# A two-layer HGRN2 and Conformer trunk on one core: weight casts gated in the inner units of the first MLP, and TensorE in written order across the seam ahead of it

## The chip, the core and the metric

The kernel runs on one core of one Trainium2 chip. The metric is the device time in microseconds (us) of one execution; the median of several runs counts. TensorE (PE) multiplies matrices, VectorE (DVE) and ScalarE (ACT) do elementwise work, GpSimd (POOL) and SyncE (SP) mostly start transfers here. Each engine has its own queue of instructions and takes it in order; an instruction waits where data of another engine is not there yet, and whatever stands behind it in that queue waits with it.

## What is computed

All arrays are float32: 1024 tokens, model width 1024, two layers. Cut to what matters:

```python
mix = hgrn2_mixer(x, ...)                                   # layer 0; layer 1: a Conformer convolution
x = layer_norm(DEEPNORM_ALPHA * x + mix, ln_mix_g[i], ln_mix_b[i])
ff = jnp.square(jax.nn.relu(x @ ffn_w1[i])) @ ffn_w2[i]     # width 1024 -> 4096 -> 1024
x = layer_norm(DEEPNORM_ALPHA * x + ff, ln_ffn_g[i], ln_ffn_b[i])
```

The HGRN2 mixer ends with an output projection, `o @ w_out`. The change lies between that projection of layer 0 and the first matrix of its MLP (the seam), and in the rest of that first matrix.

## The kernel before

**Splitting.** A float32 matrix is split into a high part, which ScalarE casts (`nc.scalar.copy`, L72 for weights, L1045 for inputs), and a low part, which VectorE subtracts from it. A product is three matmuls for each block of 128 rows: high by high, high by low, low by high (`product`, L335). A slot of 8 KB holds both parts of a 128 x 1024 block of weights.

**Forms.** The first MLP's up-projection multiplies blocks of matrices with 7 products in place of 8. Input and weights are combined into seven forms each, numbered 1 to 7; `ORDER` is 1, 2, 6, 5, 7, 3, 4. There are eight inner units `c` of the weights; each takes its seven forms in this order (`Up.form`, L1252), and one form of one unit is 2 x 12 matmuls of 512 columns. The input forms are kept in SBUF as `xf[1]` to `xf[7]`, which the order names `x1f1` to `x1f7`. The weight forms are made by `Forms.unit` (L130) from four blocks `a0` to `a3` of a unit: form 6 is `a0 + a2 + a3`, form 5 is `a2 + a3`, form 7 is `a0 + a2`, form 3 is form 6 plus `a1`, form 4 is `a3`. The weights of forms 1 and 2 of the units 0 and 1 are brought ahead of the rest (`early`, L1141) and used before it: the program runs (unit 0, form 1), (0, 2), (1, 1), (1, 2), and then the forms 6, 5, 7, 3, 4 of unit 0 and of unit 1 (L1460 to L1474). The slot at 144 KB holds the weights of (1, 2) first, and then those of (0, 6), the first form that `fw` makes (L1454).

**The seam.** The projection is computed for two halves of 512 tokens, each with four blocks `t` of 128 tokens and two halves `n` of the columns: 24 matmuls `ps<-w,oT` for each (`t`, `n`), 384 in all. Three of them, (0, 0), (1, 0) and (2, 0) of the first half, are multiplied ahead of the rest (`early_out`, L1026). VectorE adds each to the residual `y`. When both column halves of a block are there, `x1_block` (L1194) runs its norm: two statistics, an aggregate, a power on POOL (L518), and two passes of 1024 columns on VectorE. Then TensorE transposes the block in two groups of four (`ps<-ident,y`) into the two banks of `aux`. For the first half `turn` (L1096) splits the result into `xf[1]` and `xf[2]`. For the second half `x1_first` and `x1_second` (L1173, L1180) make the forms 5, 6, 7, 3 and 4 of the block from it, eight operations of 512 columns on VectorE; forms 7, 3 and 4 are kept unsplit and are split later, in pairs of 1024 columns, by `x1_late` (L1190), behind a small copy on POOL that needs the low part of the weight form at the head of the queue.

**What sets the order.** Up to the end of the HGRN2 stage all engines keep the order in which the program is written (`manual_schedule`, L371, closed at L1038). From there a scheduler orders the instructions of each engine by its own simulated clock. In the written program the transposes are `chores`: `product` runs one chore behind itself (L335 to L343), in the order in which they were appended. The chores of the last block, `x1_first(3)` and `x1_second(3)`, are appended at L1458, behind one empty chore. The scheduler is free to move them, and to move matmuls of the projection ahead of the last steps of the recurrence.

**Casts of weights split ahead.** From unit 0 on, `spare` (L1434) uses idle engines to split 38 blocks of weights of later stages. One call casts the block that the call before loaded (ScalarE, L1443), subtracts (VectorE), stores both parts, and starts the next load into the same buffer `next`, behind a copy on POOL (L1450) that needs the low part of the weight form just made. It is called from `Forms` in the first MLP's up-projection (13 of the casts lie there) and from `Slots` in the down-projection.

Of the kernel before, what the change touches and what calls it, by code (L numbers as in the profile page):

```python
# [21 lines left out]
NTB = HT // P  # L22
# [14 lines left out]
KBYTES = 220  # L37
PAIRS = [("q", 0), ("q", 1), ("q", 2), ("q", 3), ("g", 0), ("q", 4), ("q", 5), ("q", 6), ("g", 1), ("q", 7), ("g", 2), ("g", 3)]
NPOOL = (12, 11)
SEQ = "P00 P01 P02 P03 P04 P05 P06 P07 P10 P11 P12 P13 N0 P14 F0 P15 S0 P16 P17 UA0 UA1 E2 E3 N1 E4 F1 E5 E6 S1 E7 UB0 UB1 L2 L3 L4 L5 L6 L7"  # L40


# [169 lines left out]
class Background:  # L212


    def __init__(self):
        self.jobs, self.pooled, self.chores = [], [], []
        self.pe, self.dve, self.pool, self.margin, self.hold = [0.0], [0.0], [0.0], 0.0, False

    def pump(self):
# [19 lines left out]
    def flush(self, job):  # L239
        for jobs in (self.pooled, self.jobs):  # L240
            while job in jobs:
                self.step(jobs)

    def chore(self):
        if self.chores:
# [23 lines left out]
def body(ctx, tc, d, out):  # L269
# [27 lines left out]
    def slots(kbs, name):  # L297
        return ring(kbs, (2, 1024), name, F32R)

    def raws(kbs, name="raw"):  # L300
        return ring(kbs, (1024,), name)
# [33 lines left out]
    def product(ps, parts, start=True):  # L335

        n = len(parts)
        for i, ((lh, ll), (rh, rl)) in enumerate(parts):
            tensor.matmul(ps, lh, rh, start=start and i == 0, stop=False, skip_group_check=not start)
            tensor.matmul(ps, lh, rl, start=False, stop=False, skip_group_check=not start)  # L340
            tensor.matmul(ps, ll, rh, start=False, stop=i == n - 1, skip_group_check=not start)
        bg.chore()
        bg.pump()  # L343

# [691 lines left out]
    tick(100)  # L1036
    assert not waiting and not loaded and not to_load and not gates, (waiting, gates)
    order.close()  # L1038
    oT = [o[0] for o in oT]


# [152 lines left out]
    def x1_block(half, t):  # L1194
        norm(y[half][:, t, :], g, b)
        keep(half, t, y[half][:, t, :])
        if half == 0:
            bg.chores += [lambda k=k: turn(y[0][:, t, :], xf[1 + k // 4], t, k, 4) for k in (0, 4)]
            return
        if t == 0:  # L1200
            bg.done()
            late_x.update({i: view(kb, (4, HT), F32, "xl") for i, kb in ((7, 176), (3, 184))})
        if t < NTB - 1:
            bg.chores += [lambda: x1_first(t), lambda: x1_second(t)]

    for half in range(2):
        for t, n in early_out + ((0, 1), (1, 1), (3, 0), (2, 1), (3, 1)) if half == 0 else [(t, n) for t in range(NTB) for n in range(2)]:
            ps = acc()
            if half or (t, n) not in early_out:
                product(ps, wide(oT[half], t, ws[n]))  # L1210
            yv = y[half][:, t, n * HT : (n + 1) * HT]
            vector.scalar_tensor_tensor(out=yv, in0=yv, scalar=ALPHA, in1=ps, op0=ALU.mult, op1=ALU.add)
            if n == 1:
                if half == 1 and t == 0:
                    early[0].ahead(1)
                x1_block(half, t)
                if half == 0 and t:
                    bg.chore()
    for e in early[1:]:
        e.ahead(2)  # L1220

# [209 lines left out]

    hold, staged = [], []

    def spare(after):  # L1434

        if not hold:
            return
        slot, raw = hold
        now = stat.tile([P, 2, 4], F32, tag="ss", name="ss")[:, 0, :1]
        nc.vector.tensor_copy(out=now, in_=after)  # L1440
        if staged:
            key = staged.pop()
            nc.scalar.copy(out=slot[:, 0].bitcast(F32R), in_=raw)  # L1443
            vector.tensor_tensor(out=slot[:, 1].bitcast(F32R), in0=raw, in1=slot[:, 0], op=ALU.subtract)
            ready[key] = tuple(dram.tile([P, 1024], F32, name=f"ready{len(ready)}_{i}") for i in range(2))
            for i in range(2):
                nc.sync.dma_start(out=ready[key][i], in_=slot[:, i])
        if ahead:
            name, at = ahead.pop(0)
            nc.gpsimd.tensor_copy(out=raw[:, :1], in_=now)  # L1450
            nc.sync.dma_start(out=raw, in_=d[name][at])
            staged.append((name, at))

    fw = Forms(nc, vector, slots((144, 152, 48, 112, 120), "fw"), raws(run(192, 4, 4)), raws(run(160, 2, 4), "sum"), spare, 3, range(44))  # L1454
    fw.todo = [[(blocks("w1q", 0, c), 2 if c < 2 else 0)] for c in range(NFC)]
    up = Up()

    bg.chores += [lambda: None, lambda: x1_first(NTB - 1), lambda: x1_second(NTB - 1)] + [lambda: None] * 3  # L1458
    bg.chores += [lambda i=i, k=k: x1_late(i, k) for i in (7, 3, 4) for k in (0, 2)]
    up.form(0, 1, early[0].take(1)[0])  # L1460
    up.form(0, 2, early[1].take(1)[0], late=True)
# [6 lines left out]
    for c in range(NFC):  # L1468
# [5 lines left out]
            up.form(c, i, f)  # L1474
        if c in (0, 2):
            block_sums(*to_sum.pop(0), f[:2, 1, :1].bitcast(F32))
        if c == 0:
            up.settle(1)
            hold += [view(208, (2, 1024), F32, "spare"), view(216, (1024,), F32, "next")]
# [478 lines left out]
```

## Time and profile before

| | us |
|---|---|
| runs | 2061.99, 2056.68, 2056.98 |
| median | 2056.98 |
| the profiled execution | 2059.69 |
| its span, first to last instruction | 2057.9 |
| busy in it: PE, DVE, ACT, POOL | 2026.5, 1487.4, 1092.0, 392.1 |

The seam lies at about 415 to 550 us of the span, the rest of the up-projection ends near 800. A row of a timeline gives the start in us, the duration, the engine, the line, the operation, out<-in with shapes, a count where equal rows were merged, and in brackets the idle time of the engine ahead of it with what ended it. A row of the waits gives the engine, what it waited for, the total in us, the number of times, and the longest. Nearly all matmuls carry the line of the helper that records them (L204), so they are told apart by the names of their tiles. PE's matmuls overlap their neighbours: a duration of 389 ns stands for a new one every 227 ns.

### The profile page before, as it was taken

The numbers are of one execution on the slowest core, as the hardware profiler recorded it, in microseconds if no ns is written. First come the engines' busy times: TensorE is split into PE (matmuls) and PEld (weight loads), VectorE is DVE, ScalarE is ACT, GpSimd is POOL, SyncE is SP. The second block draws the span as 40 slices with busy tenths as digits, with TensorE's granted clock in tenths as the row PEclk, the third lists the DMA queues.
The fourth block names the chain that finished last, engine by engine and source line by source line (L and its number), as shares of the span: only waits on it lengthen the run. The fifth ranks groups of instructions, "written<-read, shape, count | busy, mean of one in ns | idle before, by whom it ended". The sixth has DMA issues, their size and how long they took to land. (4 is left out here: it accounts for less than half of the span.)

```text
span 2057.9 us, 29631 instructions
## 1 busy us (share of the span) xinstructions
PE 2026.5 (98%) x11144; PEld 1670.6 (81%) x11144; DVE 1487.4 (72%) x1978; ACT 1092.0 (53%) x1725; POOL 392.1 (19%) x393
## 2 busy tenths in 40 slices
PE   8999999999999999999999999999999999999998
PEld 7888887788787888888888888888888887888886
DVE  8698887877966665666567898889589666754456
ACT  5456565631654555444443776488625555443343
POOL 0112222111100000000001699079110000100002
PEclk9999999999999999999999999999999999999999
DMA  4788989842689786999998854587759778995542
GB/s 187 221 200 228 261 240 252 268 187 82 180 295 307 243 286 224 372 338 325 338 336 301 308 185 184 194 330 272 255 215 343 241 231 297 392 294 197 194 154 102
DMA packets 183944, 517.55 MB, mean 251 GB/s; under 512 B 17912, under 2 KB 49784, under 8 KB 182776
## 3 DMA queue, kind: packets, MB, share of 16 engines
q1 hardware_dynamic: 168312, 456.93, 61.8%
q0 software_dynamic: 15488, 58.72, 12.3%
q8 instruction: 87, 1.43, 0.3%
q14 instruction: 57, 0.47, 0.1%
HBM read 380.85 MB, written 201.85 MB: 283 GB/s over the span
## 5 line engine op out<-in xcount | busy, mean ns | idle before, releaser
L204 PE MATMUL ps<-dw,dh 128*128 128x512 f32 x2688 | 611.1, 389 | 0.0
L204 PEld LDWEIGHTS ps<-dw,dh 128*128 128x128 f32 x2688 | 504.2, 188 | 104.6 <-DVE dh L204 0.2
L204 PE MATMUL ps<-x1f,fw 128*128 128x512 f32 x1344 | 309.7, 392 | 4.6 <-ACT c L1266 2.5
L204 PEld LDWEIGHTS ps<-x1f,fw 128*128 128x128 f32 x1344 | 252.5, 189 | 60.3 <-ACT c L1266 3.6
L204 PE MATMUL ps<-xf,fs 128*128 128x512 f32 x1008 | 250.0, 399 | 3.7 <-issue 2.0
L204 POOL TENSOR_TENSOR cb<-cb,prod 128x512 f32<-128x512 f32 x168 | 223.1, 1337 | 12.5 <-ACT prod L1589 2.0
L204 DVE TENSOR_TENSOR dh<-dh 128x1024 fp32r<-128x1024 f32 x112 | 136.5, 1222 | 116.1 <-ACT dh L72 112.7
L204 PEld LDWEIGHTS ps<-xf,fs 128*128 128x128 f32 x1008 | 185.1, 189 | 43.3 <-issue 2.2
L204 DVE SCALAR_TENSOR_TENSOR ps<-u,par,ps 128x512 f32<-128x512 f32 x296 | 206.1, 749 | 11.0 <-ACT ps L1601 9.5
L204 PE MATMUL ps<-xa,wa 128*128 128x512 f32 x864 | 203.0, 392 | 0.1
L72 ACT CAST dh<-dh 128x1024 fp32r<-128x1024 f32 x112 | 117.4, 1051 | 156.0 <-DMA dh<-hf 148.9
L204 PEld LDWEIGHTS ps<-xa,wa 128*128 128x128 f32 x864 | 160.3, 188 | 33.2 <-ACT ha L1331 0.3
L72 ACT CAST dw<-dr 128x1024 fp32r<-128x1024 f32 x112 | 117.3, 1052 | 131.0 <-PE ps L204 115.3
L204 DVE TENSOR_TENSOR dw<-dr,dw 128x1024 fp32r<-128x1024 f32 x112 | 136.3, 1222 | 69.5 <-ACT dw L72 68.4
L1589 ACT ACTIVATE prod<-u,par 128x512 f32<-128x512 f32 x168 | 119.8, 726 | 37.1 <-POOL cb L204 36.7
L518 POOL TENSOR_TENSOR mv<-mv,nhalf 128x1 f32<-128x1 f32 x32 | 42.2, 1321 | 404.8 <-DVE mv L204 394.5
L1450 POOL COPY next<-ss 128x1 f32<-128x1 f32 x38 | 18.9, 497 | 414.5 <-DVE spare L204 255.1
L204 PE MATMUL ps<-w,oT 128*128 128x512 f32 x384 | 89.9, 392 | 1.3 <-ACT oT L932 0.8
L204 PE MATMUL ps<-xb,wa 128*128 128x512 f32 x384 | 91.1, 393 | 0.0
L204 DVE TENSOR_TENSOR spare<-next,spare 128x1024 fp32r<-128x1024 f32 x38 | 46.5, 1224 | 60.4 <-ACT spare L1443 60.3
L204 PE MATMUL ps<-vw,xf 128*128 128x512 f32 x336 | 79.9, 400 | 5.9 <-ACT vw L435 5.3
L204 PEld LDWEIGHTS ps<-w,oT 128*128 128x128 f32 x384 | 71.4, 188 | 16.6 <-ACT oT L932 1.2
(249 smaller groups left out, 2955.9 us busy)
## 6 DMA issues: line engine op xcount, KB each, us to landing
wa<-ready SPq DMA_DIRECT2D x140, 512.0 KB, 4.6
dh<-hf SPq DMA_DIRECT2D x112, 512.0 KB, 5.0
sum_w<-in_w_dram POOLq DMA_DIRECT2D x40, 1024.0 KB, 10.6
ready<-spare SPq DMA_DIRECT2D x76, 512.0 KB, 5.3
raw<-in_w1q_dram SPq DMA_DIRECT2D x66, 512.0 KB, 4.4
dr<-sum_w SPq DMA_DIRECT2D x64, 512.0 KB, 5.7
hf<-ht SPq DMA_DIRECT2D x112, 256.0 KB, 5.1
dr<-in_w_dram SPq DMA_DIRECT2D x48, 512.0 KB, 4.6
```

What stands on the lines that cost most here:

```text
L72: self.nc.scalar.copy(out=slot[:, 0, c], in_=raw[:, c])
L204: return op(*args, **kw)
L518: nc.gpsimd.tensor_tensor(out=dst, in0=src, in1=nhalf[:, :n], op=ALU.pow)
L1450: nc.gpsimd.tensor_copy(out=raw[:, :1], in_=now)
L1589: nc.scalar.activation(tp, u[:, k : k + HT], AF.Copy, scale=tap(j, k))
```

## The change

TensorE alone is put back under the written order right behind L1038, and stays there until unit 1 of the up-projection is done. So that the written order has the transposes at a useful place, they are no longer chores: `bg.soon` notes them with a due time 8.0 us later on a clock that counts TensorE's matmuls (35 matmuls), and `product` looks for due ones after every three matmuls. Each block's two groups now come together. The last block is treated as the others. In `spare`, called from the up-projection's `Forms`, a copy of one column on POOL into the slot of the high part now stands ahead of the cast, and needs the low part of the weight form just made; the down-projection's calls stay as they were.

```diff
+LAG_NORM = 8.0
...
+    def soon(self, us, *jobs):
+        self.due.append((self.pe[0] + us, jobs))
+
+    def dues(self):
+        while self.due and self.due[0][0] <= self.pe[0]:
+            for job in self.due.pop(0)[1]:
+                job()
...
             tensor.matmul(ps, ll, rh, start=False, stop=i == n - 1, skip_group_check=not start)
+            bg.dues()
...
     order.close()
+    order.enter_context(tc.manual_schedule(engines={mybir.EngineType.PE}))
...
         if half == 0:
-            bg.chores += [lambda k=k: turn(y[0][:, t, :], xf[1 + k // 4], t, k, 4) for k in (0, 4)]
+            bg.soon(LAG_NORM, lambda: turn(y[0][:, t, :], xf[1], t, 0, 4), lambda: turn(y[0][:, t, :], xf[2], t, 4, 4))
             return
         if t == 0:
-            bg.done()
+            assert not bg.due
...
-        if t < NTB - 1:
-            bg.chores += [lambda: x1_first(t), lambda: x1_second(t)]
+        bg.soon(LAG_NORM, lambda: x1_first(t), lambda: x1_second(t))
...
-                if half == 0 and t:
-                    bg.chore()
...
-    def spare(after):
+    def spare(after, late_cast=False):
...
         if staged:
             key = staged.pop()
+            if late_cast:
+                nc.gpsimd.tensor_copy(out=slot[:, 0, :1], in_=now)
             nc.scalar.copy(out=slot[:, 0].bitcast(F32R), in_=raw)
...
-    fw = Forms(nc, vector, ..., spare, 3, range(44))
+    fw = Forms(nc, vector, ..., lambda after: spare(after, True), 3, range(44))
...
-    bg.chores += [lambda: None, lambda: x1_first(NTB - 1), lambda: x1_second(NTB - 1)] + [lambda: None] * 3
+    bg.chores += [lambda: None] * 6
...
+        if c == 1:
+            order.close()
```

How the instructions move. First TensorE at the end of the recurrence, before; `ident,o` are the transposes of the last head's two halves, `xf_505` and `xf_432` are products of the last pair, `w,oT` is the projection.

```order
L204 MATMUL ps<-xf_505,fs 128x512 x6
L204 MATMUL ps<-w,oT 128x512 x6
L204 MATMUL ps<-ident,o 128x128 x4
L204 MATMUL ps<-xf_432,fs 128x512 x6
L204 MATMUL ps<-w,oT 128x512 x6
L204 MATMUL ps<-ident,o 128x128 x4
L204 MATMUL ps<-xf_432,fs 128x512 x6
L204 MATMUL ps<-w,oT 128x512 x145
L204 MATMUL ps<-ident,y 128x128 x8
```

The same place now.

```order
L205 MATMUL ps<-xf_505,fs 128x512 x6
L205 MATMUL ps<-ident,o 128x128 x4
L205 MATMUL ps<-xf_432,fs 128x512 x6
L205 MATMUL ps<-ident,o 128x128 x4
L205 MATMUL ps<-xf_432,fs 128x512 x6
L205 MATMUL ps<-w,oT 128x512 x132
L205 MATMUL ps<-ident,y 128x128 x8
```

The twelve projection matmuls that the scheduler had put between the transposes of `o` stand behind them again; the first transposes of `y` stand 36 matmuls behind the product that their norm needs (96 of the 132).

Second, TensorE where the up-projection goes from form 2 of unit 1 to the forms that `fw` makes, before; `fw_4501` holds the weights of (1, 2), `fw_5044` and `fw_5043` those of the forms 5 and 6 of unit 0.

```order
L204 MATMUL ps_70<-x1f2_4509,fw_4501 128x512 x24
L204 MATMUL ps_70<-x1f5_4505,fw_5044 128x512 x2
L204 MATMUL ps_70<-x1f6_4504,fw_5043 128x512 x4
L204 MATMUL ps_70<-x1f5_4505,fw_5044 128x512 x22
L204 MATMUL ps_70<-x1f6_4504,fw_5043 128x512 x20
```

Now, where the names have moved by one or two: `fw_4503` is (1, 2), `fw_5045` and `fw_5046` are the forms 6 and 5 of unit 0.

```order
L205 MATMUL ps_70<-x1f2_4511,fw_4503 128x512 x24
L205 MATMUL ps_70<-x1f6_4506,fw_5045 128x512 x24
L205 MATMUL ps_70<-x1f5_4507,fw_5046 128x512 x24
L205 MATMUL ps_70<-x1f7_4512,fw_5049 128x512 x24
L205 MATMUL ps_70<-x1f3_4508,fw_5051 128x512 x24
```

Form 6 now follows (1, 2) with nothing between.

Third, VectorE at the same place, before, from the first sum of unit 0's blocks on; `c1` are the evacuations of (1, 2), `x1f` the late input forms, `fw` the low parts of weight forms.

```order
L204 TENSOR_TENSOR sum_5058<-raw_5054,raw_5055 128x1024
L204 TENSOR_TENSOR fw_5050<-raw_5055,fw_5050 128x1024
L204 TENSOR_TENSOR c1_5145<-c1_5145,ps_70 128x512
L204 TENSOR_TENSOR sum_5059<-sum_5058,raw_5052 128x1024
L204 TENSOR_TENSOR raw_5054<-raw_5052,raw_5054 128x1024
L204 TENSOR_TENSOR c1_5146<-c1_5146,ps_70 128x512
L204 TENSOR_TENSOR fw_5044<-sum_5058,fw_5044 128x1024
L204 TENSOR_TENSOR fw_5043<-sum_5059,fw_5043 128x1024
```

Now, from the same sum on; the second `sum_5060` is the first sum of unit 1.

```order
L205 TENSOR_TENSOR sum_5060<-raw_5056,raw_5057 128x1024
L205 TENSOR_TENSOR sum_5061<-sum_5060,raw_5054 128x1024
L205 TENSOR_TENSOR raw_5056<-raw_5054,raw_5056 128x1024
L205 TENSOR_TENSOR fw_5046<-sum_5060,fw_5046 128x1024
L205 TENSOR_TENSOR fw_5052<-raw_5057,fw_5052 128x1024
L205 TENSOR_TENSOR fw_5049<-raw_5056,fw_5049 128x1024
L205 TENSOR_TENSOR c1_5147<-c1_5147,ps_70 128x512
L205 TENSOR_TENSOR x1f3_4508<-xl_4796,x1f3_4508 128x1024 x2
L205 TENSOR_TENSOR c1_5148<-c1_5148,ps_70 128x512
L205 TENSOR_TENSOR x1f4_4514<-x4_4490,x1f4_4514 128x1024 x2
L205 TENSOR_TENSOR sum_5060<-raw_5056,raw_5057 128x1024
L205 TENSOR_TENSOR fw_5045<-sum_5061,fw_5045 128x1024
```

The low part of form 6 (`fw_5043`, now `fw_5045`) stood second behind the last `c1`; now the two late pairs `x1f3` and `x1f4`, the low parts of the forms 4 and 7 and unit 1's sum stand ahead of it.

More of the change, by code (lines that the diff above doesn't have):

```diff
@@ L215, in __init__ @@
     def __init__(self):
-        self.jobs, self.pooled, self.chores = [], [], []
+        self.jobs, self.pooled, self.chores, self.due = [], [], [], []
         self.pe, self.dve, self.pool, self.margin, self.hold = [0.0], [0.0], [0.0], 0.0, False
@@ L1452, in spare @@
             staged.append((name, at))
-    fw = Forms(nc, vector, slots((144, 152, 48, 112, 120), "fw"), raws(run(192, 4, 4)), raws(run(160, 2, 4), "sum"), spare, 3, range(44))
+    fw = Forms(nc, vector, slots((144, 152, 48, 112, 120), "fw"), raws(run(192, 4, 4)), raws(run(160, 2, 4), "sum"), lambda after: spare(after, True), 3, range(44))
     fw.todo = [[(blocks("w1q", 0, c), 2 if c < 2 else 0)] for c in range(NFC)]
     up = Up()
-    bg.chores += [lambda: None, lambda: x1_first(NTB - 1), lambda: x1_second(NTB - 1)] + [lambda: None] * 3
+    bg.chores += [lambda: None] * 6
     bg.chores += [lambda i=i, k=k: x1_late(i, k) for i in (7, 3, 4) for k in (0, 2)]
```

## The prediction

> **What bounds the kernel now.** I read the page's busy shares first, then TensorE's waits by stretch, then the timeline of the stretches that the edit touches.
>
> ```profile
> PE 2026.5 (98%) x11144; PEld 1670.6 (81%) x11144; DVE 1487.4 (72%) x1978; ACT 1092.0 (53%) x1725; POOL 392.1 (19%) x393
> ```
>
> TensorE is busy 2026.5 of 2057.9 us, so the whole kernel has 31 us of idle TensorE, and an edit that only reorders can win a part of these or add to them. TensorE's waits in three stretches (seam, then the inner units of the first MLP):
>
> ```profile
> PE ps L204 <- ACT fw L72: 1.5, 1, 1.5
> PE ps L204 <- DVE c L204: 0.3, 1, 0.3
> ...
> PE ps L204 <- ACT c L1266: 1.8, 2, 1.3
> ...
> PE ps L204 <- ACT c L1266: 0.5, 1, 0.5
> PE ps L204 <- DVE c L204: 0.2, 1, 0.2
> ```
>
> The first two lie at 420 to 545 us (the seam), the third at 620 to 700, the last two at 700 to 800. So the seam wait is 1.8 us and the inner units lose 2.5 us. That is all that these two edits can remove directly.
>
> The idle costs more than its length. Windows (start:end, length, PE busy, count, granted clock, DMA share, GB/s) and two rows of the PE timeline:
>
> ```profile
> 347.45 1.08 PE L204 MATMUL ps<-xf,fs 128*128 128x512 f32 x4 [2.02 <-issue]
> ...
> 350.00:352.00 2.00, 2.00 (x6) 0.50 1.06 248
> ...
> 536.86 0.70 PE L204 MATMUL ps<-x1f,fw 128*128 128x512 f32 x2 [0.28 <-DVE c L204]
> 539.04 11.19 PE L204 MATMUL ps<-x1f,fw 128*128 128x512 f32 x41 [1.48 <-ACT fw L72]
> ...
> 540.00:542.00 2.00, 2.00 (x6) 0.50 0.46 135
> 542.00:544.00 2.00, 2.00 (x8) 0.66 1.04 383
> ```
>
> After 2.02 us of idle, and after 0.28 + 1.48 = 1.76 us, the granted clock stood at 0.50 for about 3.4 us (540 to 542 wholly, 542 to 544 at 0.66, which is 1.36 us at half), so each lost 1.7 us more. After 1.25 us (659 us, below) it did not.
>
> **Part 1, TensorE in written order at the end of the recurrence.** In the trace:
>
> ```profile
> 413.28 1.62 PE L204 MATMUL ps<-xf,fs 128*128 128x512 f32 x6
> 415.70 0.73 PE L204 MATMUL ps<-w,oT 128*128 128x512 f32 x2 [0.80 <-ACT oT L932]
> 416.96 1.20 PE L204 MATMUL ps<-w,oT 128*128 128x512 f32 x4 [0.52 <-DVE oT L204]
> 417.99 0.60 PE L204 MATMUL ps<-ident,o 128*128 128x128 f32 x4
> ...
> 421.54 1.64 PE L204 MATMUL ps<-xf,fs 128*128 128x512 f32 x6
> 423.01 33.06 PE L204 MATMUL ps<-w,oT 128*128 128x512 f32 x145
> 455.91 1.03 PE L204 MATMUL ps<-ident,y 128*128 128x128 f32 x8
> 456.70 6.39 PE L204 MATMUL ps<-w,oT 128*128 128x512 f32 x27
> ```
>
> The unit costs: (455.91 - 423.01) / 145 = 0.227 us for a matmul, 456.70 - 455.91 = 0.79 us for eight transposes. Now the order puts the four transposes of `o` directly behind the six matmuls that start at 413.28, whose slots end at 414.65. What they wait for:
>
> ```profile
> 416.05 1.16 ACT L741 ACTIVATE o<-ps,ss 128x128 f32<-128x128 f32 x4
> ...
> 418.52 1.20 ACT L741 ACTIVATE o<-ps,ss 128x128 f32<-128x128 f32 x4
> ...
> 423.90 0.69 DVE L204 SCALAR_TENSOR_TENSOR t<-ps,sq 128x512 f32<-128x512 f32 x1 [0.90 <-ACT sq L854]
> ```
>
> These ScalarE rows stand in the same order in both programs and wait for nothing that TensorE does after 414.65. So the transposes start at 417.3 instead of a filler at 415.70: 2.65 us of idle. Four transposes (0.36) and six matmuls (1.37) bring 419.0; the next `o` is there at 419.75, 0.75 idle; then six matmuls end at 421.5. Six `w,oT` matmuls later one waits for the evacuation of the last pair's bank: 424.59 (the VectorE row's end) - 422.90 (421.54 + 6 x 0.227) = 1.7 us behind the pair's last matmul, 1.4 of them filled, 0.35 idle. So the stretch stands as if it had begun at 421.9 with nothing done. Before, it began at 423.0 with 12 matmuls done, which is as if at 420.3. Loss: 1.6 us.
>
> Idle of 2.65 us in one piece is more than the 2.02 that halved the clock, so I take a half clock at about 417 to 420.5. It overlaps the 0.75 and part of the 0.35 above and adds only 0.7: the stretch begins as if at 422.6.
> [...]
>
> **Part 2, the transposes 35 matmuls behind their norm.** Number the matmuls from there, so that 384 end the output projection. For the first half nothing waits: from its add of 478.95 (rows below) to the end of its last step a norm takes 482.42 + 1.28 - 478.95 = 4.75 us, and 35 matmuls take 8. In the second half VectorE also does the eight form steps for each token block. Its order up to the first matmul with a low part of form 6 (after matmul 482) decides. From the add of block 3, columns 0, which needs matmul 360, VectorE's new order holds 18 operations of 1024 columns, 24 of 512 or of that cost, and two tiny ones. Rows for the prices (VectorE timeline):
>
> ```profile
> 478.95 0.68 DVE L204 SCALAR_TENSOR_TENSOR y<-y,ps 128x512 f32<-128x512 f32 x1
> ...
> 482.42 1.28 DVE L204 SCALAR_TENSOR_TENSOR y<-y,mv,ln_mix_b 128x1024 f32<-128x1024 f32 x1 [0.44 <-POOL mv L518]
> ...
> 529.37 0.69 DVE L204 TENSOR_TENSOR y<-y,x1f 128x512 f32<-128x512 f32 x1
> 530.10 0.69 DVE L204 SCALAR_TENSOR_TENSOR y<-y,ps 128x512 f32<-128x512 f32 x1
> 530.75 0.69 DVE L204 TENSOR_TENSOR x1f<-y,x1f 128x512 fp32r<-128x512 f32 x1
> 531.36 0.68 DVE L204 SCALAR_TENSOR_TENSOR x<-y,x1f 128x512 f32<-128x512 f32 x1
> ...
> 545.29 4.63 DVE L204 TENSOR_TENSOR x1f<-xl,x1f 128x1024 fp32r<-128x1024 f32 x4 [1.16 <-ACT x1f L1045]
> ```
>
> 4.63 / 4 = 1.16 us each for 1024 columns; starts 0.73 apart where one needs the one before and 0.61 where not, I take 0.63 for 512. So 18 x 1.16 + 24 x 0.63 = 36.0, plus 0.35 for the two tiny ones, 0.45 for the POOL power in the last norm and 0.2 for the last transposes: 37.0 us in which VectorE has no gap to give. TensorE reaches matmul 360 at 422.6 + 360 x 0.227 + 6 x 0.79 = 509.1, VectorE starts 0.2 later, and the low part is there at 546.3; TensorE takes it at 546.4. TensorE alone would be at matmul 480 at 422.6 + 109.0 + 8 x 0.79 = 537.9. On the way the last group of transposes waits for its norm, by the same count some 1.4 us; this wait lies inside the 37.0.
>
> The cause at the end is one queue. Form 6's weights go into the slot that form 2 of unit 1 still reads; before, TensorE spent two matmuls of form 5 there and waited 1.48 us. Now ScalarE's cast of form 6 stands behind four casts of late input forms, and VectorE's low part stands behind `c1`, the `x1f4` pair and the next unit's sum. `c1` itself waits for matmul 480. So even a VectorE that is on time needs 0.6 + 2 x 1.16 + 1.14 + 1.22 + 0.3 = 5.6 us behind matmul 480, and TensorE has two matmuls (0.45) to put there: at least 5.1 us idle, against 1.76 before.
>
> In the trace two matmuls of the new form were done at 539.04. So this place is reached 546.4 - 539.04 = 7.4 us later, part 1 included. The half clock behind it was there before (1.7 us) and I take the same. Behind it, forms 5, 7, 3, 4 have 24 matmuls (5.5 us) each, and VectorE catches up.
>
> **Part 3, the gated casts.** Rows at the longest wait, ScalarE and TensorE, then a VectorE row, then ScalarE's waits at 560 to 780:
>
> ```profile
> 656.68 1.05 ACT L1443 CAST spare<-next 128x1024 fp32r<-128x1024 f32 x1 [4.28 <-DMA next<-in_wpw_dram]
> ...
> 659.21 3.06 PE L204 MATMUL ps<-x1f,fw 128*128 128x512 f32 x12 [1.25 <-ACT c L1266]
> ...
> 708.09 1.23 DVE L204 TENSOR_TENSOR spare<-next,spare 128x1024 fp32r<-128x1024 f32 x1 [5.06 <-ACT spare L1443]
> ...
> ACT spare L1443 <- DMA next<-in_wpw_dram: 29.3, 10, 4.3
> ```
>
> ScalarE takes its queue in order: it held the copy of `c`, and so TensorE, behind a cast whose weights had not landed. The gate puts the cast behind a POOL copy that needs the low part of the current form; by then the load of one `spare` call earlier is long in. ScalarE then waits for VectorE's copy and POOL's, about 1 us, and a copy of `c` has a whole form (5.5 us) of cover. The added POOL copies cost POOL little (19% busy). Queued behind the cast are VectorE's `spare` subtract, which now stands one or two rows behind its gate and idles VectorE some 1.6 us each time, and the stores on SP; before, VectorE waited up to 5.06 us for the same cast. I take the full 2.5 us gain; bounds 0 and 2.5.
>
> **The sum.** +7.4 - 2.5 = +4.9 us. The profiled execution took 2059.69 (span 2057.9), 2.7 above the median of the runs, 2056.98; nothing in the sum scales with that, so a profiled execution would take 2064.6 and the median 2062. A measurement of this kernel tells about 0.3% (6.2 us) from no change: below 2050.8 or above 2063.2.
>
> **The rivals.**
> - *The clock stays full at 417*: a gap of 2.65 us does not halve it, part 1 costs 1.6 instead of 2.3, and the time is 2061.3. For it: the 0.80 + 0.52 us of idle at 415.70 did not. Against: 2.02 did. Chance 0.12. [...]
> - *VectorE is on time at the seam*, since single operations overlap better than my 0.63 and 1.16. Then only the floor holds: part 1 with 2.3, the seam 5.1 - 1.76 = 3.3, the casts -2.5: +3.1, and 0.7 less if the clock stays full; 2059.8. Against it: VectorE's starts in the quoted rows are as tight as its durations. Chance 0.18.
> - *A load is late, the slower side.* The next unit's sum, which now stands ahead of form 6's low part, needs two blocks whose buffers come free only with the low parts of forms 4 and 7, at about 538. Until 544, when VectorE reaches the sum, is 6 us. From a landing of over 6 us every microsecond goes straight to TensorE. DMA issues, KB each and median us to landing:
>
> ```profile
> sum_w<-in_w_dram POOLq DMA_DIRECT2D x40, 1024.0 KB, 10.6
> ...
> raw<-in_w1q_dram SPq DMA_DIRECT2D x66, 512.0 KB, 4.4
> ```
>
>   The loads in question are the second row; the first, of 1 MB, goes out next to them and is the upper end. So up to +4.6, taken as +3, 2065. Chance 0.20.
> - *The gate wins nothing*: ScalarE waits for POOL as long as it did for the load. Then 2064.5. Against it: POOL is idle there. Chance 0.10.
> - Both edits help and the seam wait vanishes (1.76 + 1.7 + 2.5 = 6.0 us, 2051): the order of VectorE excludes it, 0.02.
>
> **The numbers.** The forecast has 0.38 (2060 to 2063.5; 0.06 of it above the bound). Slower by over 0.3%: 0.06 + 0.20 + 0.10 = 0.36. Faster: 0.02. The rest, 0.62, is within 0.3%. Range: the forecast, the clock's rival and the gate's (0.60), most of the on-time case and half of the late load (0.23): 2057.5 to 2066.5.
>
> **What would show it.** TensorE's timeline after: transposes of `o` with some 2.6 us of idle on ScalarE ahead of them; a granted clock of 0.5 behind them; one wait of 1 to 2 us at the last group of `ident,y` on VectorE; at the first matmuls of form 6 two waits, on ScalarE's cast and on VectorE's low part, together 5 to 7.5 us; no wait for `c` over 0.5 us after 620. The forecast is wrong if the seam's two waits are under 4 us together, or if ScalarE's waits at the gated cast bring TensorE's `c` waits back.

## The result and the profile after

| | before | after |
|---|---|---|
| median of the runs, us | 2058.55 (22 runs, 2054.10 to 2065.14) | 2063.74 (22 runs, 2059.63 to 2071.63) |
| profiled execution, us (span) | 2059.69 (2057.9) | 2063.70 (2061.9) |

The ratio of after to before is 1.0023 (95% interval 1.0015 to 1.0032): 4.7 us slower, inside the 0.3% that one measurement can hardly tell. The forecast was +4.9 us and 2062.0, range 2057.5 to 2066.5. The median of before is 1.6 us above that of the three runs shown first, so it is the difference that compares.

TensorE's timeline of after (start, length, operation, and in brackets the idle time ahead of it and what ended it):

```profile
416.11 0.66 PE L205 MATMUL ps<-ident,o 128*128 128x128 f32 x4 [2.36 <-ACT o L751]
...
421.42 30.49 PE L205 MATMUL ps<-w,oT 128*128 128x512 f32 x132
...
525.13 1.09 PE L205 MATMUL ps<-ident,y 128*128 128x128 f32 x8 [1.59 <-DVE y L205]
525.98 13.87 PE L205 MATMUL ps<-x1f,fw 128*128 128x512 f32 x60
542.60 0.73 PE L205 MATMUL ps<-x1f,fw 128*128 128x512 f32 x2 [2.75 <-ACT fw L73]
546.64 13.74 PE L205 MATMUL ps<-x1f,fw 128*128 128x512 f32 x52 [3.31 <-DVE fw L205]
```

The four foretold waits are there: 2.36 us for the last head's output (2.65 in the forecast, which counted from the end of a matmul's slot and not from the end of its row), 1.59 at the last transposes, 2.75 + 3.31 at form 6. Windows of after (start:end, length, busy TensorE, count, granted clock, DMA share, GB/s) show a half clock behind the first, and another that began at about 543.4 us, inside the last two waits (542 to 544 us has 0.85), and went on behind them:

```profile
416.00:418.00 2.00, 1.89 (x9) 0.78 1.00 389
418.00:420.00 2.00, 2.00 (x8) 0.50 1.03 422
...
546.00:548.00 2.00, 1.36 (x3) 0.50 0.86 240
548.00:550.00 2.00, 2.00 (x6) 0.50 1.04 307
```

VectorE's timeline of after, the two ends of the chain that was counted at 37.0 us: from the add of block 3 at 509.00 to the end of form 6's low part at 546.59 it is 37.6.

```profile
509.00 0.69 DVE L205 SCALAR_TENSOR_TENSOR y<-y,ps 128x512 f32<-128x512 f32 x1 [0.57 <-PE ps L205]
...
541.96 2.35 DVE L205 TENSOR_TENSOR x1f<-x,x1f 128x1024 fp32r<-128x1024 f32 x2
...
545.37 1.22 DVE L205 TENSOR_TENSOR fw<-sum,fw 128x1024 fp32r<-128x1024 f32 x1
```

In the inner units, 560 to 840 us, TensorE's waits came down to one row; ScalarE's at the casts (in total, times, longest) moved from the load to GpSimd. The forecast had about 1 us for each; they took 24.2 / 7 = 3.5 us on average:

```profile
PE ps L205 <- DVE c L205: 0.2, 1, 0.2
```

```profile
ACT spare L1453 <- POOL spare L1452: 24.2, 7, 6.8
...
ACT spare L1453 <- DMA next<-in_wpw_dram: 8.1, 3, 4.6
```

**How single profiles are compared here.** The part ahead of 412 us is the same in all these kernels, yet from one execution to the next it ends up to 9 us apart. So I use two distances that don't hang on it. A goes from the moment when the last head's scaled output is ready (where TensorE starts its transposes; in the scheduler's order 0.06 us behind the end of ScalarE's row) to the third matmul of form 6 in unit 0. B goes from there to the first matmul of the down-projection (`dw,dh`). Where form 6 starts without a wait, its third matmul is worked out: 62 matmuls of 0.227 us (13.87 us less the 0.48 that one takes to drain, over 59) behind the start of the row that follows the last transposes, or 53 with the longer lag.

| kernel | A | B | A+B against before | timed ratio, 95% interval |
|---|---|---|---|---|
| before | 121.8 | 288.8 | | |
| after | 130.5 | 284.7 | +4.6 | 1.0023 (1.0015 to 1.0032) |
| casts only | 121.8 | 286.7 | -2.2 | 0.9990 (0.9978 to 1.0002) |
| written order only | 130.6 | 284.1 | +4.1 | 1.0019 (1.0007 to 1.0031) |
| after, later `o` | 129.7 | 284.9 | +3.9 | 1.0013 (1.0001 to 1.0024) |
| after, slots exchanged | 123.5 | 289.6 | +2.5 | 1.0000 (0.9989 to 1.0012) |
| after, 44 matmuls | 125.5 | 287.0 | +1.9 | 1.0002 (0.9991 to 1.0012) |
| both repairs (slots, later `o`) | 123.0 | 285.1 | -2.5 | 0.9983 (0.9971 to 0.9995) |
| slots exchanged, no gate | 123.6 | 291.2 | +4.1 | 1.0014 (1.0002 to 1.0026) |
| both repairs, sums later | 123.0 | 283.4 | -4.3 | 0.9975 (0.9963 to 0.9987) |
| before, gate, sums later | 121.8 | 286.6 | -2.3 | 1.0008 (0.9995 to 1.0020) |
| both repairs, sums later, 44 | 121.5 | 284.2 | -4.9 | 0.9977 (0.9966 to 0.9987) |
| both repairs, sums later, no gate | 123.1 | 290.4 | +2.9 | 1.0019 (1.0008 to 1.0031) |
| the same, load's copy on VectorE | 123.0 | 283.7 | -4.0 | 0.9986 (0.9975 to 0.9998) |

A+B, from one profile each, follows the timed ratio (0.001 is 2.1 us) within about 2.5 us in all rows but one, taken up below. So after's 4.7 us are A + 8.8 and B - 4.1. A half clock of 3.41 us in one of these distances makes it 1.7 us longer: before and after both have one behind the start of form 6, in B; casts only (granted clock 1.00 from 536 to 552 us), both repairs, both repairs with the sums later (with 35 and with 44 matmuls) and the last row (in these four a matmul every 0.227 us from the last transposes on) have none.

### The profile page after: what moved, and what is told of

Its sections match the earlier page's. It is cut to its first block, busy times and chain, and to the rows that moved or that the text cites. A ratio compares the mean times of both kernels' runs of the same rounds, so it can differ in the third digit from the quotient of the medians.

```text
span 2061.9 us, 29644 instructions
## 1 busy us (share of the span) xinstructions
PE 2026.0 (98%) x11144; PEld 1672.5 (81%) x11144; DVE 1489.5 (72%) x1978; ACT 1096.1 (53%) x1725; POOL 395.7 (19%) x405
## 5 line engine op out<-in xcount | busy, mean ns | idle before, releaser
L205 PEld LDWEIGHTS ps<-xb,wa 128*128 128x128 f32 x384 | 71.1, 188 | 14.3
L205 PEld LDWEIGHTS ps<-vw,xf 128*128 128x128 f32 x336 | 64.6, 193 | 20.4 <-ACT vw L445 5.3
```

The source lines that it names most:

```text
L205: return op(*args, **kw)
```

## The experiments

**Each half alone.** Casts only is the kernel before with this edit alone; written order only is after without it:

```diff
+            if late_cast:
+                nc.gpsimd.tensor_copy(out=slot[:, 0, :1], in_=now)
             nc.scalar.copy(out=slot[:, 0].bitcast(F32R), in_=raw)
```

> The kernel before with the gate on the casts and nothing else. In the trace of after, the stretch from the third matmul of form 6 in unit 0 to the first matmul of the down-projection took 831.3 - 546.6 = 284.7 us, against 827.9 - 539.0 = 288.9 before: 4.2 us less, where the forecast had 2.5. Theory A, the gate alone does this: the stretch takes 284.7, no wait for c over 0.3 us after 620 us, and the time is 4.2 us (0.2%) below before, a ratio of 0.998. Theory B, the gate is worth the 2.5 us of listed waits and the other 1.7 us came with TensorE's written order: the stretch takes 286.4, ratio 0.9988. Rival C, the gate wins nothing since ScalarE waits for GpSimd instead: the stretch takes 288.9, ratio 1.000.

> The changed kernel without the gate on the casts: only TensorE's written order and the later transposes. Theory A: form 6's third matmul in unit 0 at 546.6 as in after, 7.6 us later than before; the waits for c come back (2.8 us listed) and the stretch to the down-projection takes 288.9, so the time is 7.6 us above before, ratio 1.0037. Theory B: the stretch takes 287.2, plus 5.9 us, ratio 1.0029. Rival: with TensorE in written order the units no longer wait for c at all, the stretch takes 284.7 and the time is that of after, plus 3.4 us.

TensorE's timeline of written order only, from 540 to 840 us:

```profile
543.93 1.04 PE L205 MATMUL ps<-x1f,fw 128*128 128x512 f32 x2 [2.74 <-ACT fw L73]
547.97 284.23 PE L205 MATMUL ps<-x1f,fw 128*128 128x512 f32 x1246 [3.01 <-DVE fw L205]
832.04 8.32 PE L205 MATMUL ps<-dw,dh 128*128 128x512 f32 x36
```

Without any gate 1246 matmuls ran with no listed wait. On the written order the gate wins nothing: B is 284.1 without it, 284.7 with it, and timed 1.0019 against 1.0023, inside each other's intervals. So the 4.1 us of after's B are not the gate's; the rival named for the second run holds for B.

On the kernel before, the gate alone made B 286.7, the size of theory B. But TensorE's timeline of casts only still has the waits:

```profile
538.07 11.58 PE L204 MATMUL ps<-x1f,fw 128*128 128x512 f32 x48 [1.47 <-ACT fw L72]
551.08 108.61 PE L204 MATMUL ps<-x1f,fw 128*128 128x512 f32 x478 [1.44 <-ACT c L1266]
660.00 5.74 PE L204 MATMUL ps<-x1f,fw 128*128 128x512 f32 x24 [0.31 <-ACT c L1266]
666.83 158.06 PE L204 MATMUL ps<-x1f,fw 128*128 128x512 f32 x696 [1.09 <-DVE c L204]
```

The waits for `c` are 2.8 us here, against 2.5 listed before. Of the 2 us by which B is shorter, 1.7 are the half clock that before had behind the start of form 6 (0.50 from 540 to 542 us) and this execution did not have (1.00 there). The timed ratio, 0.9990 (0.9978 to 1.0002), can't be told from 1 either. So no run shows that the gate wins anything on the kernel before.

**Is it the place of the transposes of `o`?** They stand six matmuls later:

```diff
-            for c in range(half * NTB, half * NTB + NTB):
-                tensor.transpose(out_ps[:, c, :], o[:, c], ident)
+            def turn_out():
+                for c in range(half * NTB, half * NTB + NTB):
+                    tensor.transpose(out_ps[:, c, :], o[:, c], ident)
+                later(1, end)
...
-            later(1, end)
+            later(2 if h == H - 1 else 0, turn_out)
```

> The changed kernel with the two groups of transposes of the last head's output each put six matmuls later in TensorE's order. The forecast's part 1: what the written order costs there is the place of the transposes. Then TensorE waits 1.3 us (12 matmuls end at 416.0, the output is scaled at 417.3) and 0.75 us, the clock stays full since no gap is over 1.6 us, and the matmuls of the output projection begin at 420.1 on the scale of before instead of 421.4 in after; since VectorE's chain at the seam starts from a matmul of this projection, all of it comes 1.3 us earlier: 1.3 us below after, ratio to after 0.9994. Rival 1: the two gaps together still halve the clock: 0.6 us below after. Rival 2: something other than TensorE sets the seam's end: form 6 at the same 546.6 as in after.

TensorE's timeline of it:

```profile
414.68 0.66 PE L205 MATMUL ps<-ident,o 128*128 128x128 f32 x4 [0.98 <-ACT o L751]
...
417.18 0.66 PE L205 MATMUL ps<-ident,o 128*128 128x128 f32 x4 [0.45 <-ACT o L751]
417.60 1.62 PE L205 MATMUL ps<-w,oT 128*128 128x512 f32 x6
420.50 3.74 PE L205 MATMUL ps<-w,oT 128*128 128x512 f32 x15 [1.28 <-DVE t L205]
```

The clock stayed full there: the six matmuls behind the first wait took 1.64 us (415.09), against 2.40 in after (416.52). The stretch of the projection began 2.4 us earlier behind the output (417.60 - 414.68 = 2.9 us, against 421.42 - 416.11 = 5.3 in after); the expected 1.3 set a time of after beside one of before, whose output is ready 1.2 us later. The wait for the last pair's bank, which grew to 1.28 us, took more than half of the 2.4 back, and A fell by 0.9. So what TensorE saves at 417 does reach the end of the seam, through VectorE's start. The timed ratios, 1.0013 and 1.0023, don't settle it: their intervals overlap.

**Is it the slot, or VectorE's chain?**

```diff
-slots((144, 152, 48, 112, 120), "fw")
+slots((152, 144, 48, 112, 120), "fw")
```

> The changed kernel with the first two of the five weight slots exchanged, so that form 6 of unit 0 goes into the slot whose raw weights were cast long before, and form 5 into the one that form 2 of unit 1 reads until matmul 480. Theory: the seam's two waits (2.75 and 3.3 us) come from this slot and from what VectorE and ScalarE have queued ahead of form 6; now its low part stands ahead of both copies of c1 and is ready at about 537.5, so form 6 starts without a wait, its third matmul at about 540.2 instead of 546.6, and the half clock behind is gone: 6.4 + 1.7 = 8 us below after, ratio to before 0.9977. Form 5's low part is there at about 544.6, needed at 545. Rival 1, VectorE's chain of 37 us is the bound whatever the slots: the wait moves to form 5 or form 3, and the time is at most 3 us below after. Rival 2, the loads behind the slots come late: same, with waits on DMA in VectorE's rows.

VectorE's timeline of it, then TensorE's:

```profile
535.91 1.22 DVE L205 TENSOR_TENSOR fw<-sum,fw 128x1024 fp32r<-128x1024 f32 x1
...
542.78 1.22 DVE L205 TENSOR_TENSOR fw<-sum,fw 128x1024 fp32r<-128x1024 f32 x1
```

```profile
524.73 54.68 PE L205 MATMUL ps<-x1f,fw 128*128 128x512 f32 x240
579.84 8.47 PE L205 MATMUL ps<-x1f,fw 128*128 128x512 f32 x36 [0.44 <-ACT c L1274]
588.59 65.60 PE L205 MATMUL ps<-x1f,fw 128*128 128x512 f32 x288 [0.28 <-DVE c L205]
656.63 12.81 PE L205 MATMUL ps<-x1f,fw 128*128 128x512 f32 x48 [2.45 <-ACT c L1274]
670.51 158.05 PE L205 MATMUL ps<-x1f,fw 128*128 128x512 f32 x696 [1.07 <-DVE c L205]
```

The low part of form 6 was done at 537.1 and form 5's at 544.0, and TensorE ran on without a wait: A fell by 7.0 us, 0.5 of it because the clock also stayed full at 417 (1.00 in all windows of 2 us from 412 to 424 us). So the seam's wait came from the slot that form 2 of unit 1 still read, with what stood ahead of form 6 on ScalarE and VectorE because of it. But B rose by 4.9 us: waits for `c` of 4.2 us came back, with the gate in place. The longest, 2.45 us, stands behind VectorE: it had waited 4.87 and 2.30 us, up to 645.49 and 650.75, for stores of `ht` (`hf<-ht`), and its adds to `c`, which ScalarE needs, came late. The time fell by 0.23% where 0.46% was expected.

**Is the distance of 35 matmuls too short?**

```diff
-LAG_NORM = 8.0
+LAG_NORM = 10.0
```

> The changed kernel with the transposes 44 matmuls behind their norm instead of 35. In after, TensorE waits 1.59 us at the last group, and form 6's low part comes 37.6 us behind the add at matmul 360 with no gap on VectorE. Theory, VectorE's chain sets the seam's end: the same operations stand behind the add at matmul 360, but those that read block 2's transposes now wait for TensorE (the transposes come 9 matmuls, 2.1 us, later, at about 513.6 to 514.7 on the scale of after, where VectorE is at 512.5), so the last norm and form 6's low part come about 2 us later: the wait at the last group stays at 1.6 us, form 6's third matmul is at about 548.7 instead of 546.6, and the time is 2 us above after, ratio to before about 1.003. Rival, the distance is too short: the wait at the last group vanishes and form 6 starts 1.6 us earlier, ratio about 1.0015.

VectorE's timeline of it, then TensorE's:

```profile
513.71 0.68 DVE L205 SCALAR_TENSOR_TENSOR y<-y,ps 128x512 f32<-128x512 f32 x1
...
544.36 1.22 DVE L205 TENSOR_TENSOR fw<-sum,fw 128x1024 fp32r<-128x1024 f32 x1
545.50 2.35 DVE L205 TENSOR_TENSOR x1f<-xl,x1f 128x1024 fp32r<-128x1024 f32 x2
```

```profile
530.01 1.09 PE L205 MATMUL ps<-ident,y 128*128 128x128 f32 x8 [0.68 <-DVE y L205]
...
543.83 0.73 PE L205 MATMUL ps<-x1f,fw 128*128 128x512 f32 x2 [1.14 <-ACT fw L73]
545.63 4.60 PE L205 MATMUL ps<-x1f,fw 128*128 128x512 f32 x12 [1.07 <-DVE fw L205]
```

Both my expectation (A + 2) and its rival (A - 1.6) failed: A fell by 5.0 us. I had taken it that the same operations stand ahead of form 6's low part. They don't: with the other lag the scheduler put the pairs of late input forms (2.35 us each, the last row above) behind it, and the chain from the add of block 3 is 31.9 us (545.58 - 513.71) instead of 37.6. That VectorE's queue sets form 6's start holds; its length is a matter of order.

**Is the gain paid back in the inner units, and by whom?** Three kernels: both repairs together; the exchanged slots without the gate; and both repairs with the block sums moved:

```diff
-        if c in (0, 2):
+        if c in (4, 6):
             block_sums(*to_sum.pop(0), f[:2, 1, :1].bitcast(F32))
```

> The changed kernel with both repairs, the exchanged weight slots and the later transposes of the last head's output; the gate stays. At the seam: from the first of the six matmuls that open the end of the recurrence to the third matmul of form 6 some 126.7 us, against 134.5 in after, 127.6 with the slots alone and 125.8 before. Theory A, what the seam saves is paid back in the inner units, whose copies of c then wait for a crowded DMA: waits for c of 3 to 5 us between 560 and 690, the stretch from form 6's third matmul to the down-projection near 289, ratio to before 1.000 as with the slots alone. Theory B, the waits for c in that run were chance: the stretch is 285, ratio 0.998.

> The exchanged weight slots without the gate on the casts: neither the seam's wait nor the gate. It fills the fourth place beside after (wait and gate, waits for c 0.2 us), the written order alone (wait, no gate, 0.0 us) and the exchanged slots (gate, no wait, 4.3 us). Theory A, the units' waits for c are set by the lead that the seam's wait gives the other engines and the DMA, and the gate is worth about 2 us where there is no lead: waits for c of 5 to 7 us, the stretch from form 6's third matmul to the down-projection at 291, ratio to before 1.001. Rival, the gate itself is what holds ScalarE in the run with the exchanged slots: waits for c under 1 us, stretch 285, ratio 0.998.

> The kernel with both repairs and the gate, and the two block sums of units 0 and 2 (1 MB copies and accumulating transfers on GpSimd's and SyncE's queues) put to units 4 and 6 instead. In the run with the exchanged slots the DMA engines were at a share of 1.0 from 630 to 660 us, ahead of the wait of 2.45 us for c. Theory, the crowd of transfers is what makes the inner units wait when TensorE comes early: with these transfers gone from 560 to 680 the waits for c there fall below 1 us, the stretch from form 6's third matmul to the down-projection takes 285 or less, and the time is 4 to 5 us below the kernel with both repairs, ratio to before 0.997 to 0.998. Rival 1: the waits move to units 4 to 6 with the transfers, and the time is the same as with both repairs. Rival 2: the stores of the down-projected halves and the casts alone fill the queues: waits for c in 560 to 680 as without this edit.

Both repairs: A 123.0, waits for `c` of only 1.6 us in all, ratio 0.9983, the first version that beats the kernel before. The 4.2 us of waits with the exchanged slots alone seem to be in part the chance of that execution. Without the gate it was as theory A had it: B 291.2 and one wait of 5.65 us for `c`. VectorE's and ScalarE's timelines ahead of that wait, then ScalarE's of written order only:

```profile
653.18 0.69 DVE L205 SCALAR_TENSOR_TENSOR ht<-ht,hr 128x512 f32<-128x512 f32 x1 [5.79 <-DMA hf<-ht]
```

```profile
661.69 1.04 ACT L1453 CAST spare<-next 128x1024 fp32r<-128x1024 f32 x1 [2.77 <-DMA next<-in_wpw_dram]
```

```profile
662.40 1.05 ACT L1453 CAST spare<-next 128x1024 fp32r<-128x1024 f32 x1 [3.99 <-DMA next<-in_wpw_dram]
```

Two delays add up to the 5.65 us: VectorE's wait for a store, which held up the copies of `c`, and a late load at ScalarE's cast. Written order only has the same late cast, 0.7 us later, and TensorE did not wait, since it had come to the third matmul of form 6 5.2 us later (547.97 against 542.75). So the seam's wait is a lead that hides these delays. Beside written order only, which has no gate either, the exchanged slots took 7.0 us from A and added 7.1 to B: all of it was paid back, and the timed ratios, 1.0014 and 1.0019, don't differ. With the sums later the last waits in 560 to 690 went, B is 283.4 and the ratio 0.9975. Its interval overlaps that of both repairs, so this last step is likely, not shown.

**Three ways to the same units.** The kernel before with the gate and the sums later; the best one with the lag of 44 matmuls; and the best one without the gate.

> The kernel before, with TensorE in the scheduler's order, with the gate on the casts and the two block sums put from units 0 and 2 to units 4 and 6. Distances that don't hang on when the program's first part ends: from the last head's scaled output to the third matmul of form 6, 121.7 us in before and in casts only, 130.5 in after, 123.1 with both repairs; from there to the down-projection 288.9 in before, 286.7 in casts only, 283.3 with both repairs and the sums later. Theory, the crowd of transfers in units 0 and 2 is what makes the units wait, whatever TensorE's order: the second distance falls to 283.5 and the sum of both to 405.3, 5.3 us under before, ratio 0.9974; so the old order at the seam with these two edits is as fast as the best so far. Rival, the units are quick only in the written order: the second distance stays at 286.7, ratio 0.999.

> The kernel with both repairs, the gate and the sums later, with the transposes 44 matmuls behind their norm instead of 35. With 35 TensorE waited 1.61 us at the last group; with 44 matmuls and the old slots it waited 0.68. Theory: form 6 no longer waits in either, so this time the 0.95 us at the last group reach the seam's end: from the last head's scaled output to form 6's third matmul 122.1 us instead of 123.05, the rest as with 35, ratio to before 0.997. Rival: the later transposes push VectorE's late steps so far that form 6 or form 5 waits again: 123 us or more, ratio 0.9975 or above.

> The kernel with both repairs and the sums later, without the gate on the casts. With the sums in units 0 and 2 the gate was worth 291.1 - 289.5 = 1.6 us of the stretch from form 6's third matmul to the down-projection (exchanged slots, without and with gate). Theory A, the gate only mends what the crowd of transfers brings about, since without it the loads land before their casts are reached: the stretch is 283 to 284 as with the gate, waits for c under 0.6 us, ratio to before 0.9975. Theory B, ScalarE still stands behind a cast whose load is late once in a while: waits for c of 1.5 to 3 us, stretch 285 to 286.5, ratio 0.9985 to 0.999.

On the kernel before the later sums won no time. Its waits for `c` are 1.59 us (at 732.7, where the sums now run) instead of the 2.8 of casts only, but B is 286.6, since this execution had the half clock behind the start of form 6 (0.50 from 540 to 542 us), 1.7 us. Its timed ratio, 1.0008, is 4 us above what A+B says; that one stays open. With 44 matmuls A came down by 1.5 us, where 0.95 was foretold (121.5; the wait at the last transposes 0.36 us), but B rose by 0.9 and the time is the same. Without the gate neither theory's size held: 5.67 us of wait for `c`. The rows ahead of it show its cause. ScalarE's, GpSimd's, SyncE's and TensorE's timelines:

```profile
726.60 1.04 ACT L1455 CAST spare<-next 128x1024 fp32r<-128x1024 f32 x1 [10.67 <-DMA next<-in_wpw_dram]
```

```profile
710.24 0.86 POOL L433 DMA_DIRECT2D sum_w<-sum_w  x1 [11.74 <-DMA sum_w<-in_w_dram]
718.83 0.81 POOL L433 DMA_DIRECT2D sum_w<-sum_w  x1 [7.73 <-DMA sum_w<-sum_w]
719.37 0.46 POOL L1462 COPY next<-ss 128x1 f32<-128x1 f32 x1
```

```profile
719.86 0.34 SPq L1463 DMA_DIRECT2D next<-in_wpw_dram  x1
```

```profile
729.12 102.81 PE L205 MATMUL ps<-x1f,fw 128*128 128x512 f32 x444 [5.67 <-ACT c L1276]
```

The load `next` goes out only when GpSimd has made a copy of one column, and that copy stood in GpSimd's queue behind an accumulating transfer that waited 7.73 us for the transfer before it. The load is late, ScalarE stands at its cast, and `c` behind it. GpSimd's timeline of the kernel before has the same rows ahead of TensorE's longest wait for `c`:

```profile
644.94 0.83 POOL L423 DMA_DIRECT2D sum_w<-sum_w  x1 [7.78 <-DMA sum_w<-sum_w]
645.48 0.48 POOL L1450 COPY next<-ss 128x1 f32<-128x1 f32 x1
```

**The test of that cause.** No gate, and that copy on VectorE in the first MLP's units:

```diff
-            nc.gpsimd.tensor_copy(out=raw[:, :1], in_=now)
+            (nc.vector if late_cast else nc.gpsimd).tensor_copy(out=raw[:, :1], in_=now)
             nc.sync.dma_start(out=raw, in_=d[name][at])
```

> The kernel with both repairs and the sums later and no gate on the casts, with one more edit: the small copy ahead of each load of the next spare weights, which holds that load back, runs on VectorE instead of GpSimd, in the first MLP's units. In the run without this edit TensorE waited 5.67 us for c at 729 us: ScalarE's cast waited 10.67 us for the load, which went out at 719.9, since GpSimd's copy stood from about 710 to 719.4 behind a sum's accumulating transfer that waited 7.73 us for the transfer before it. The same row stands before the waits of 5.65 us (exchanged slots without gate) and of 1.25 us (the kernel before, GpSimd's copy at 645.5 behind a wait of 7.78). Theory, the late load comes from GpSimd's queue and not from a slow transfer: without that queue the wait at 729 goes below 1 us, the stretch from form 6's third matmul to the down-projection takes 283 to 284.5 us instead of 290.3, and the ratio to before is 0.997 to 0.998 instead of 1.0019, without a gate. Rival, the transfers themselves are slow beside the sums: the wait stays at 3 us or more, ratio 1.000 to 1.002. Rival 2: the copy on VectorE waits for ScalarE's cast of the same buffer and delays VectorE: waits for c on VectorE of over 1 us.

SyncE's, GpSimd's and TensorE's timelines of it:

```profile
707.85 0.77 SPq L1461 DMA_DIRECT2D next<-in_wpw_dram  x1
```

```profile
715.24 0.81 POOL L433 DMA_DIRECT2D sum_w<-sum_w  x1 [8.97 <-DMA sum_w<-sum_w]
```

```profile
811.44 11.17 PE L205 MATMUL ps<-x1f,fw 128*128 128x512 f32 x48 [0.83 <-ACT c L1276]
```

GpSimd's second transfer still waits 8.97 us, but the load goes out at 707.85, ahead of it. The 5.67 us are gone, B is 283.7 as with the gate, and the time went from 1.0019 to 0.9986, where 0.997 to 0.998 was expected. What is left are the 0.83 us and, outside of B, 0.76 us at the start of the down-projection. Some of the scheduler's order on VectorE changed with the edit. So this wait of 5.67 us comes from GpSimd's queue, and with the copy off that queue the kernel without a gate is as fast as the one with it, inside the intervals (0.9986 and 0.9975). Not every wait for `c` comes from there: those of 2.45 and 5.65 us with the exchanged slots stand behind VectorE's waits for stores, the second only in part. That the gate works by keeping ScalarE from standing at the late load is argued here, not shown.

## Why the prediction was right, point by point

The number was right (+4.9 against +4.7), in part by luck: the seam cost 8.8 us instead of 7.4, and the inner units gave back 4.1 instead of 2.5, two misses that cancel. The first two parts were right in mechanism, and the third was right in sign for another reason than the one given.

- *Part 1, 2.3 us.* The stretch of the output projection began 5.3 us behind the output's readiness (421.42 - 416.11). The forecast had 5.3 with the wait for the last pair's bank counted in; this wait lies inside the row of 132 matmuls, which is 30.49 us long where 131 x 0.227 + 0.48 make 30.2, so 0.3 us. The half clock cost 0.5 of the 0.7 counted: from the output to the first transposes of `y` it is 451.75 - 416.11 = 35.6 us, and 450.43 - 415.33 = 35.1 with the exchanged slots, where the clock stayed full. That it came at all was chance, as the windows below show: of the five kernels with this order at 417, all with a gap of 2.34 to 2.36 us, three had it (after, written order only, 44 matmuls: the six matmuls behind it took 2.40 to 2.81 us) and the two with the exchanged slots had not (1.64 us).
- *Part 2, the seam.* Forecast: A = 546.4 - 417.3 = 129.1; measured 130.5. From the stretch's start to VectorE's add it took 87.6 us instead of 86.7. Of this 0.3 is the bank's wait, and 0.5 are the six groups of transposes, which take 0.88 us each and not the 0.79 counted: a row of 48 matmuls has its transposes 499.76 - 488.77 = 10.99 us behind its start, 0.09 more than 48 x 0.227. The chain took 37.6 instead of 37.0. That the wait at the last transposes lies inside the chain was right as a count, but the claim that VectorE's order fixes the seam's end was too strong: with other slots, or another lag, the same work stands in another order, and 5 to 7 us go.
- *Part 3, the gated casts.* This step failed: "the full 2.5 us gain" for the gate. B fell by 4.1, and by 4.8 with no gate at all. Nor did ScalarE's waits at the casts shrink to about 1 us each: those listed above are 24.2 + 8.1 = 32.3 us, against the 29.3 for the load before. Where TensorE comes about 9 us late to form 6, loads, casts and GpSimd are that much ahead, and the waits for `c` don't arise; where it comes early they return, 0.5 to 4.2 us with the gate and 2.5 to 5.9 without. So about half of the seam's 8.8 us comes back by itself, and the two terms of my sum are not independent. The argument that GpSimd is little used (19% busy) failed too: it stood for 7 to 12 us at a time in front of a transfer, which no busy share shows.
- *The rivals.* The late load at the seam did not happen: no wait on a DMA stands in VectorE's rows there. The gate that wins nothing (0.10) came true in this kernel, with its reason: ScalarE waited as long as before. TensorE did not, because of the lead. The clock that stays full at 417 came true in other executions.

The half clock is less regular than the prediction had it. TensorE's timeline of the exchanged slots:

```profile
415.33 0.66 PE L205 MATMUL ps<-ident,o 128*128 128x128 f32 x4 [2.36 <-ACT o L751]
```

The same 2.36 us that halved the clock in after did not here (1.00 from 412 to 424 us), and the 0.28 + 1.48 us that halved it in before did not in casts only (0.28 + 1.47, and 1.00 from 536 to 552 us).

Four traces show where half clocks begin. In each, those that can be placed begin whole multiples of 3.413 us apart: at 348.79 and 539.93 us in before (56 of them), at 348.85, 417.12 and 543.41 in after (20 and 37), at 271.1, 417.9 and 544.2 in written order only (43 and 37), and at 656.6 and 1141.3 with the exchanged slots (142); in the last two traces the places are worked out from the mean clock of windows of 2 us. Windows of this length with their edges on these multiples, of before, of after and of the exchanged slots:

```profile
536.52:539.94 3.42, 1.66 (x7) 1.00 0.46 153
```

```profile
413.70:417.12 3.42, 1.06 (x8) 1.00 0.93 334
```

```profile
410.87:414.28 3.41, 2.10 (x13) 1.00 0.66 216
414.28:417.69 3.41, 2.05 (x10) 1.00 0.89 333
```

In before and in after the idle time lies in one window, 3.42 - 1.66 = 1.76 and 2.36 us of it, and the next window runs at 0.50. With the exchanged slots the edge at 414.28, 71 x 3.413 ahead of the half clock at 656.6, cuts the wait in two, the two windows have 1.31 and 1.36, and the clock stays full. For casts only the place of the windows is not shown. Not counting the one at each program's end, the traces of before and after have five half clocks (one of them 6.83 us long), and all begin behind a window with 1.76 us of idle TensorE or more. Of the 1186 other windows at full clock behind the first 11 us of these two traces, one has 1.76 us or more (1.93, in before at 2048.63).

## What to carry to other kernels

A wait on the critical engine is also a lead for all the others: before a seam's stall is priced, or removed, look at what runs short behind it, and price the two together. A copy that only holds back a transfer belongs on an engine whose queue does not wait for other transfers (here that took 5.67 us of TensorE's waits away); a busy share of 19% says nothing about that. And a chain counted on an engine whose order a scheduler makes is a bound for this order alone: the exchange of two slots took 7 us out of it, and with both repairs and the sums later the change became 0.25% faster than the kernel before instead of 0.23% slower.

## What the runs showed of the hardware

- In the traces of before and after TensorE's granted clock fell to 0.50 for 3.41 us, or for 6.83 (after, from 543.41), behind a window of a 3.41 us grid in which TensorE was idle for 1.76 to 2.68 us: five of the six such windows at full clock, not counting each program's end. A gap of 2.34 to 2.36 us ahead of the transposes of `o` halved the clock in three executions and not in two; in after it lay in one window, with the exchanged slots the grid cut it into 1.31 and 1.05 us. An estimate from these numbers: if the grid falls anywhere, a single gap of 2.36 us has 1.76 us in one window in (3.41 - 2.36 + 2 x 0.60) / 3.41 = 0.66 of the executions (three of five here), so on average its half clock costs two thirds of the 1.7 us that 3.41 us at half take.
- A transfer instruction in GpSimd's queue that waited 7.73 us for an earlier transfer held up the copy behind it (719.37 us, both repairs with the sums later and no gate), and through it a load (out at 719.86) and TensorE (5.67 us).
- The same first 412 us ended up to 9 us apart from one execution to the next (the last output ready at 414.2 to 423.0), as much as any edit here moved. In the profiles only distances inside one execution could be compared.
